# SyncE's transfers in program order, modulation weights loaded beside attention and the FFN's output, and W fetched by DMA in both forms, in a two-layer encoder trunk

## The chip, the core and the metric

The kernel runs on one core of a Trainium2 chip. The metric is the device time of one execution in microseconds (us); less is better. The engines are PE (TensorE), DVE (VectorE), ACT (ScalarE), POOL (GpSimd) and SP (SyncE, which here only issues DMAs). Each engine works through its own instructions in order.

## The reference

Two request groups of 256 tokens each (one row of 512 tokens in the kernel) go through two layers:

```python
mod = silu(c) @ w_mod + b_mod                    # 1024 x 6144 weights per layer; sh1, sc1, gt1, sh2, sc2, gt2
h  = rmsnorm(x, ln1_g) * (1 + sc1) + sh1
q_down, kv_down, rg_x, rg_gate, gdn_qkv, gdn_z, gdn_alpha, gdn_beta, gates = split_cols(h @ w_in)
o_mla, o_rg, o_gdn = attention(q_down, kv_down), rglru(rg_x, rg_gate), gated_delta(gdn_qkv, ...)
x  = x + gt1 * (sum_n sigmoid(gates[n]) * (o_n @ w_branch[n])) @ w_out
h2 = rmsnorm(x, ln2_g) * (1 + sc2) + sh2
x  = x + gt2 * (silu(u_gate) * u_lin) @ ffn_w_down   # u = dwconv(h2 @ ffn_w_up)
```

The gated delta branch (4 heads, both directions, chunks of 64) needs, for each chunk, the inverse T of a unit lower triangular matrix: `T = solve(eye + A, eye)`, then `u = T @ (v * beta)` and `w = T @ (kb * exp(g))`.

## The kernel before

All activations lie feature by token (128 x 512 tiles). Weights are float32; each is split into a rounded part wh and a rest wl, and each product takes three PE passes (hh*wh, hl*wh, hh*wl).

**The weight stream.** The units of all jobs (128x128 weight blocks) lie one behind the other in `wall`; eight units are one chunk of 512 KB. `prefetch` (L375) loads a chunk into one of `NRAW = 3` buffers named raw, `split_chunk` (L381) has ACT cast it to wh (L387) and DVE subtract to wl (L388, recorded as L298), six units before PE needs it. A raw buffer comes free when wl is written.

**The order of the work.** Python code walks the table `BRANCHES` of jobs and writes PE's instructions in that order (`tc.manual_schedule` for PE, L231). A `Driver` keeps a clock `now` that only PE's own work advances. Side tasks are generators: each yields a time to sleep (from `SLACK`) or an event, and `poll` continues those that are due between matmuls. `until(event)` is used where a job must not be written before an event's time: while that time has not come, it runs the tasks that are due and, with none due, puts `now` forward to the next time that a task waits for.

```python
            wakes = [w[0].t if isinstance(w[0], Event) else w[0] for w in self.tasks] + [ev.t]
            wakes = [w for w in wakes if w is not None and w > self.now]
            self.now = min(wakes)
```

Job uk.0 (keys of attention) begins with `drv.until(ev_ckv)`, and that event is set by `ev_ckv.set(SLACK["low_rank_out"])`, which is 152.5. The orders of DVE, ACT, POOL and SP are chosen by a scheduler of the framework, which puts an instruction where it expects it to be ready.

**Modulation (w_mod).** `mod_gen` (L441) computes the columns of mod in groups of blocks: per 512 KB tile, four narrow matmuls with csil (128x32), `PE.matmul(ps..., csil, src)`. Blocks 4 to 9 of a layer (24 tiles) run beside the delta-rule stage; the task is spawned at job close, sleeps `SLACK["mod1"]` for each tile and loads the tile into a raw buffer (L483), so it shares the three buffers and SP with the weight stream. Blocks 10 and 11 are loaded as oraw beside the output projection, blocks 0 and 1 of the next layer run beside the FFN's input (up), and blocks 2 and 3 at the layer's end from tiles hraw that take the place of h.

**The delta-rule stage.** After attention (job close), `GDN.solve` (L1312) runs once per head as a side task. PE computes the Gram matrices (gdn_gram), DVE and POOL make from them B and the diagonal blocks cb. Then a chain of small steps inverts the 16x16 diagonal blocks: SP writes cb to DRAM (dl, L1380) and reads it back in another layout (Lb, four DMAs, L1386); POOL does 30 dependent steps on X (L1387 to L1393; recorded as L292 and L298); SP writes X to DRAM (dx, four DMAs, L1397) and reads it back as W (L1401, L1402); DVE transposes both halves (L1403, L1404). X has one buffer and is set to its start value by a DMA that ACT issues (L1383). The task then sleeps `SLACK["X"]` and `combine` (L1417) has PE build larger blocks (gdn_l16, gdn_l32, gdn_l64), run the recurrence (gdn_rec) and the output (gdn_o).

Of the kernel before, what the change touches and what calls it, by code (L numbers as in the profile page):

```python
# [8 lines left out]
F32 = mybir.dt.float32  # L9
# [4 lines left out]
ALU = mybir.AluOpType  # L14
# [4 lines left out]
P = 128  # L19
T = 512  # L20
# [22 lines left out]
def jobs():  # L43
# [22 lines left out]
    "rg_all": 16.0, "ssq": 6.5, "kq": 8.0, "norm": 2.8, "normed": 17.0, "mod1": 8.0, "mod2": 8.9,  # L66
    "kd": 0.1, "start": 0.6, "diag2": 4.6, "cq": 2.1, "lr_diag": 5.3, "diag": 30.4}
# [159 lines left out]
def body(tc, xT, cT, wall, wmod, pvec, fng, cst, rope, xinit, yT, dbg=None):  # L227
    nc = tc.nc
    es = ExitStack()
    with es:  # L230
        es.enter_context(tc.manual_schedule(engines={mybir.EngineType.PE}))  # L231
        _body(es, tc, nc, xT, cT, wall, wmod, pvec, fng, cst, rope, xinit, yT, dbg)


def _body(es, tc, nc, xT, cT, wall, wmod, pvec, fng, cst, rope, xinit, yT, dbg):
# [36 lines left out]
    V.memset(tiny, 1e-30)  # L272
    dx = [dp.tile([8, P, 32], F32, name=f"dx{i}", tag=f"dx{i}", bufs=1) for i in range(2)]


    def later(pool):
        nc.sync.dma_start(rt_, rope)
        nc.sync.dma_start(fg, fng)
        zero = pool.tile([P, 8, 32], F32, name="zero")
        G.memset(zero, 0.0)  # L280
        for t in dx:
# [93 lines left out]
    def prefetch(at):  # L375
# [61 lines left out]

    def mod_gen(l, groups, pace):  # L441
        if l not in mods:
# [32 lines left out]
        for blocks in groups:  # L475
            n = len(blocks)
            w = 4 // n
            ps = aux_tile(name="mod")
            for i in range(4 * n):
                raw = loaded.pop((l, 4 * blocks[0] + i), None)  # L480
                if raw is None:
                    raw = wp.tile([P, UC * P], F32, name="raw", tag="raw", bufs=NRAW)
                    nc.sync.dma_start(raw, wmod[l, 4 * blocks[0] + i])  # L483
                    yield pace
                half, i4 = divmod(i, 2 * n)
                for e in range(4):
# [7 lines left out]
                yield 0.0  # L494
# [194 lines left out]
    for l in range(depth):  # L689
# [338 lines left out]


        last = l + 1 == depth  # L1030
        for job in JOBS:
            k, *ix = job
            state["job"] = k
            if k == "in6":
# [10 lines left out]
                ev_cq.set(SLACK["cq"])  # L1045
                drv.spawn(low_rank())
            elif k in ("gq", "gk", "gv"):
                if k == "gq" and ix[0] >= 2:
# [23 lines left out]
            elif k == "close":  # L1072
                for t in range(8):
                    debug(f"K{t}_{l}", Kt[:, t, :])
                    debug(f"Q{t}_{l}", Qt[:, t, :])
                fill(mp, 1888)
                mstack.close()
                RT, RS = 8, 2
# [3 lines left out]
                for hd in range(4):  # L1082
                    drv.spawn(gdn.solve(hd))
                drv.spawn(mod_gen(l, ((4, 5, 6, 7), (8, 9)), SLACK["mod1"]))
            elif k == "x":
# [14 lines left out]
            elif k == "mid":  # L1100
                drv.until(gdn.ev_o)
                fill(gdn.g2, 1952)
                g2stack.close()
# [3 lines left out]
            elif k == "close2":  # L1107
# [5 lines left out]

                def oraw(i):
# [3 lines left out]
                preload(l, (10, 11), oraw)  # L1118
                drv.spare.append([0.0, mod_gen(l, ((10, 11),), 0.0)])
            elif k == "out3":  # L1120
# [22 lines left out]
            elif k == "up3":  # L1143
                for n, ps in enumerate(gemms(hs(h2), 3)):
                    up(ps, n)
                if not last:
                    drv.spawn(mod_gen(l + 1, ((0, 1),), SLACK["mod2"]))
            elif k == "up":
                up(gemm(hs(h2)), ix[0])
            elif k == "down":  # L1150
                d, g = ix
                if d == 0:
                    sq = Norm(fp, 3)
                    if not last:
# [3 lines left out]
                        def hraw(i):  # L1158
                            half = []
                            for e in range(2):  # L1160
                                tag = "h%s%d" % ("hl"[e], i % 8)
                                t = hp.tile([P, T], F32, name="hraw", tag=tag)
                                nc.sync.dma_start(t, wmod[l + 1, i][:, e * T:(e + 1) * T])
                                half.append(t)
                            return tuple(half)
                        preload(l + 1, (2, 3), hraw)
                ps = gemm(acts, g)
# [14 lines left out]
        if not last:  # L1182
            drv.spare.append([0.0, mod_gen(l + 1, ((2, 3),), 0.0)])
# [14 lines left out]
class GDN:  # L1198
# [113 lines left out]
    def solve(self, h):  # L1312
# [75 lines left out]
        for j in range(15):  # L1388
# [4 lines left out]
            self.sub(X[:, :, j + 1:], X[:, :, j + 1:], tmp[:, :, :n], G)  # L1393
        dx = self.dx[h % 2]
        for o in range(4):
            e, w = o // 2, 16 * (o % 2)
# [3 lines left out]
        W = g2.tile([P, 2, 2, 4, 32], F32, name="W", tag="W", bufs=1)  # L1400
# [9 lines left out]
        for d in range(2):  # L1410
            self.mul(at[d], at[d], C(inc[d]).unsqueeze(1).to_broadcast([P, 4, P]), G)
        yield SLACK["X"]
        if h:
            yield self.ev_free[h - 1]
# [286 lines left out]
```

## Time and profile before

| | |
|---|---|
| median of 3 runs | 2037.99 us (2036.72 to 2038.59) |
| the profiled execution | 2037.11 us, span from first to last instruction 2035.3 us |
| PE busy | 1956.5 us (96%), mean granted clock 0.978 |
| DVE, ACT, POOL busy | 1246.0, 818.7, 250.9 us |
| DMA | 229.99 MB, mean 113 GB/s |

A busy PE is not a fast PE: the granted clock of a stretch is read beside its busy time. An in-order engine that waits holds everything that is queued behind the waiting instruction, so the views to read are those that say what a queue stood at.

### The profile page before, as it was taken

How to read it: one execution, taken by the hardware profiler on the slowest of the kernel's cores; microseconds unless marked ns; L12 is line 12 of the kernel's file. 1: busy time of each engine (PE TensorE's matmuls, PEld its weight loads, DVE VectorE, ACT ScalarE, POOL GpSimd, SP SyncE). 2: the span in 40 equal slices, each digit the busy share in tenths (PEclk: the TensorE clock that was granted, in tenths of full speed). 3: DMA queues.
4: the chain of work that ended last, by engine and by line, in shares of the span. 5: the costliest groups of instructions: out<-in, count | busy, mean ns of one | idle time of the engine just before them, and what ended most of it. 6: DMA issues, size and time to landing. Idle time of an engine off the chain costs nothing.

```text
span 2035.3 us, 29431 instructions
## 1 busy us (share of the span) xinstructions
PE 1956.5 (96%) x11563; PEld 1568.4 (77%) x11563; DVE 1246.0 (61%) x2354; ACT 818.7 (40%) x1275; POOL 250.9 (12%) x495
## 2 busy tenths in 40 slices
PE   9999977999999999999999998799999999999998
PEld 5777755768888778888878786577788888888887
DVE  5775766745466766663367847685544667666534
ACT  3453454433233444442244533563323344444322
POOL 1100343132100100000011003513130010000000
PEclk9999988999999999999999998899999999999999
DMA  7232333334235343344333123233442633233233
GB/s 300 93 83 69 104 94 89 110 119 120 87 127 185 122 128 102 104 161 127 121 111 113 52 85 104 77 110 91 130 114 82 209 102 103 94 93 104 94 97 111
DMA packets 114138, 229.99 MB, mean 113 GB/s; under 512 B 52304, under 2 KB 57552, under 8 KB 114000
## 3 DMA queue, kind: packets, MB, share of 16 engines
q1 hardware_dynamic: 107376, 219.98, 34.8%
q10 hardware_dynamic: 6624, 8.14, 1.2%
q8 instruction: 91, 1.49, 0.3%
q14 instruction: 47, 0.39, 0.1%
HBM read 221.00 MB, written 7.08 MB: 112 GB/s over the span
## 4 chain that ended last, share of the span: by engine, by line
PE 84%; POOL 5%; DVE 4%; DMA 3%; issue 2%; ACT 1%; SPq 1%; POOLq 0%; DVEq 0%; ACTq 0%
PE mm_up L220 24%; PE mm_down L220 12%; PE mm_gate L220 11%; PE mm_br L220 6%; PE mm_out L220 4%; PE mm_in L220 3%; PE mm_z L220 2%; PE mm_gk L220 2%; PE mod L220 2%; POOL X L298 2%; POOL xt L292 2%; PE mm_gq L220 2%; PE mm_gv L220 2%; PE att_s L220 1%; PE gdn_rec L220 1%
## 5 line engine op out<-in xcount | busy, mean ns | idle before, releaser
L298 DVE TENSOR_TENSOR wl<-raw,wh 128x1024 fp32r<-128x1024 f32 x304 | 375.1, 1234 | 309.7 <-ACT wh L387 296.8
L387 ACT CAST wh<-raw 128x1024 fp32r<-128x1024 f32 x304 | 319.0, 1050 | 539.9 <-PE mm_down L220 129.2
L220 PE MATMUL mm_up<-hh,wh 128*128 128x512 f32 x704 | 276.7, 393 | 3.4 <-POOL hh L308 3.4
L220 PE MATMUL mm_up<-hl,wh 128*128 128x512 f32 x704 | 275.2, 391 | 0.0
L220 PE MATMUL mm_up<-hh,wl 128*128 128x512 f32 x704 | 275.0, 391 | 0.0
L301 DVE SCALAR_TENSOR_TENSOR cv<-mm_up,pv,cv 128x510 f32<-128x510 f32 x176 | 131.2, 748 | 67.9 <-ACT cv L552 64.8
L220 PE MATMUL mm_gate<-hh,wh 128*128 128x512 f32 x384 | 160.6, 418 | 0.0
L220 PEld LDWEIGHTS mm_up<-hh,wh 128*128 128x128 f32 x704 | 132.9, 189 | 34.6 <-POOL hh L308 3.9
L220 PEld LDWEIGHTS mm_up<-hl,wh 128*128 128x128 f32 x704 | 132.9, 189 | 27.8 <-DVE hl L298 0.3
L220 PEld LDWEIGHTS mm_up<-hh,wl 128*128 128x128 f32 x704 | 132.9, 189 | 27.6
L220 PE MATMUL mm_gate<-hh,wl 128*128 128x512 f32 x384 | 150.3, 391 | 0.0
L220 PE MATMUL mm_gate<-hl,wh 128*128 128x512 f32 x384 | 149.9, 390 | 0.0
L220 PE MATMUL mm_down<-ah,wl 128*128 128x512 f32 (+1 forms) x396 | 144.8, 366 | 0.5 <-DVE wl L298 0.5
L220 PE MATMUL mm_down<-ah,wh 128*128 128x512 f32 (+1 forms) x396 | 144.9, 366 | 0.0
L220 PE MATMUL mm_down<-al,wh 128*128 128x512 f32 (+1 forms) x396 | 144.7, 365 | 0.0
L308 POOL TENSOR_SCALAR hh<-hn 128x256 fp32r<-128x256 f32 x64 | 34.1, 545 | 681.2 <-ACT hn L569 678.8
L552 ACT ACTIVATE cv<-mm_up,pv 128x512 f32<-128x512 f32 x88 | 68.5, 780 | 93.7 <-PE mm_up L220 93.7
L220 PEld LDWEIGHTS mm_gate<-hh,wh 128*128 128x128 f32 x384 | 72.2, 188 | 19.5 <-issue 6.5
L220 PEld LDWEIGHTS mm_gate<-hh,wl 128*128 128x128 f32 x384 | 72.1, 188 | 16.3 <-DVE wl L298 0.2
L220 PEld LDWEIGHTS mm_down<-ah,wl 128*128 128x128 f32 x396 | 74.7, 189 | 12.8 <-DVE wl L298 0.7
L220 PEld LDWEIGHTS mm_down<-al,wh 128*128 128x128 f32 x396 | 74.7, 189 | 12.0
L220 PEld LDWEIGHTS mm_down<-ah,wh 128*128 128x128 f32 x396 | 74.7, 189 | 12.0
(388 smaller groups left out, 3853.2 us busy)
## 6 DMA issues: line engine op xcount, KB each, us to landing
raw<-in_wall_dram SPq DMA_DIRECT2D x304, 512.0 KB, 3.5
raw<-in_wmod_dram SPq DMA_DIRECT2D x56, 512.0 KB, 3.7
mraw<-in_wmod_dram SPq DMA_DIRECT2D x16, 512.0 KB, 9.9
oraw<-in_wmod_dram SPq DMA_DIRECT2D x16, 512.0 KB, 6.9
hraw<-in_wmod_dram SPq DMA_DIRECT2D x16, 256.0 KB, 6.1
x<-in_xT_dram SPq DMA_DIRECT2D x8, 256.0 KB, 5.5
xr<-in_xT_dram ACTq DMA_DIRECT2D x8, 256.0 KB, 3.3
xdram<-x ACTq DMA_DIRECT2D x16, 128.0 KB, 2.2
```

The lines of the kernel that those rows point to most:

```text
L220: return self.pe.matmul(out, lhsT, rhs, **kw)
L292: (eng or V).tensor_tensor(out, a, b, ALU.mult)
L298: (eng or V).tensor_tensor(out, a, b, ALU.subtract)
L301: V.scalar_tensor_tensor(out, a, s, b, op0, op1)
L308: G.tensor_scalar(hi, x, 1.0, 0.0, ALU.mult, ALU.add)
L387: A.copy(wh, raw)
L552: A.activation(dst, ps, AF.Identity, bias=bias, scale=w[lo])
```

## The change

Five things, in the words of the code. (1) SP joins PE under the manual order, so its DMAs go out in the order in which the Python code writes them. (2) `split_chunk` loads the chunk two further on. (3) `solve` yields before each of its transfers (cb 4.0, dl 2.5, X 18.0, dx 3.0, W 3.0 in place of X 28.0), so that their place in SP's order is set by the driver's clock; X gets two buffers, and its start value is loaded once per layer (xi) and copied by POOL; POOL also writes a reordered copy XT; X and XT go to two DRAM tensors, and all four parts of W come by DMA, so the two DVE transposes go. (4) The 24 modulation tiles of blocks 4 to 9 go to a task spawned at job in6, beside attention, with a pool of their own of two buffers (mraw) and `SLACK["mod1"]` 5.0; a tile's buffer is reloaded after its matmuls. (5) Blocks 0 and 1 of the next layer move from beside up to beside down, in hraw tiles, with `SLACK["mod2"]` 8.0.

```diff
-    "modev": 0.7, ..., "gram": 3.1, "X": 28.0, ... "mod1": 8.0, "mod2": 8.9,
+    "modev": 0.7, ..., "gram": 3.1, "cb": 4.0, "dl": 2.5, "X": 18.0, "dx": 3.0, "W": 3.0, ... "mod1": 5.0, "mod2": 8.0,
-        es.enter_context(tc.manual_schedule(engines={mybir.EngineType.PE}))
+        es.enter_context(tc.manual_schedule(engines={mybir.EngineType.PE, mybir.EngineType.SP}))
     def split_chunk(at):
             raw = prefetch(at)
             loads.pop(at)
+            l, i = divmod(at[0] * NCH + at[1] + 2, NCH)
+            if l < depth:
+                prefetch((l, i))
+    def modulation(l, groups, pace, tile_of, ahead):
+        todo = [4 * g[0] + i for g in groups for i in range(4 * len(g))]
+        def load():
+            if todo:
+                i = todo.pop(0)
+                loaded[l, i] = tile_of(l, i)
+        for _ in range(ahead):
+            load()
+        return mod_gen(l, groups, pace, load)
-                raw = loaded.pop((l, 4 * blocks[0] + i), None)
-                if raw is None:
-                    raw = wp.tile([P, UC * P], F32, name="raw", tag="raw", bufs=NRAW)
-                    nc.sync.dma_start(raw, wmod[l, 4 * blocks[0] + i])
+                if load is not None:
                     yield pace
+                raw = loaded.pop((l, 4 * blocks[0] + i))
...
+                if load is not None:
+                    load()
+        def mla_raw(l, i):
+            raw = rp.tile([P, UC * P], F32, name="mraw", tag="mraw", bufs=2)
+            nc.sync.dma_start(raw, wmod[l, i])
+            return raw
             if k == "in6":
                 drv.spawn(low_rank())
+                drv.spawn(beside(modulation(l, ((4, 5, 6, 7), (8, 9)), SLACK["mod1"], mla_raw, 2)))
             elif k == "close":
+                drv.until(ev_mod)
-                drv.spawn(mod_gen(l, ((4, 5, 6, 7), (8, 9)), SLACK["mod1"]))
+                gdn.xi = gdn.g2.tile([P, 8, 16], F32, name="xi", tag="xi")
+                nc.sync.dma_start(gdn.xi, xinit)
             elif k == "up3":
-                if not last:
-                    drv.spawn(mod_gen(l + 1, ((0, 1),), SLACK["mod2"]))
             elif k == "down":
-                        preload(l + 1, (2, 3), hraw)
+                        drv.spawn(ahead())
# solve
+        yield SLACK["cb"]
         nc.sync.dma_start(dl.rearrange("t p c -> p t c"), cb)
+        yield SLACK["dl"]
-        X = g2.tile([P, 8, 16], F32, name="X", tag="X", bufs=1)
-        nc.scalar.dma_start(X, self.xinit)
+        X = g2.tile([P, 8, 16], F32, name="X", tag="X", bufs=2)
+        XT = g2.tile([P, 16, 8], F32, name="XT", tag="XT", bufs=1)
+        G.tensor_scalar(X, self.xi, 1.0, 0.0, ALU.mult, ALU.add)
...
-            nc.sync.dma_start(dx.rearrange("t (q s c) i -> s (t q) c i", s=2, c=16)
-                              [o % 2][:, 8 * e:8 * e + 8, w:w + 16], X[32 * o:32 * o + 32])
-        nc.sync.dma_start(W[:, 1, 0], dx[0:4].rearrange("t p c -> p t c"))
-        nc.sync.dma_start(W[:, 0, 1], dx[4:8].rearrange("t p c -> p t c"))
-        V.transpose(W[:, 0, 0], W[:, 1, 0])
-        V.transpose(W[:, 1, 1], W[:, 0, 1])
+        G.tensor_scalar(XT.rearrange("p r c -> p c r"), X, 1.0, 0.0, ALU.mult, ALU.add)
         yield SLACK["X"]
+        for t, (b, n) in zip(dx, ((X, 8), (XT, 16))):
+            for o in range(4):
+                nc.sync.dma_start(v[:, c:c + 8, w:w + 16] if n == 8 else v[:, :, w + c:w + c + 8], b[32 * o:32 * o + 32])
+        yield SLACK["dx"]
+        for i in range(2):
+            nc.sync.dma_start(W[:, 1 - i, 0], dx[i][0:4].rearrange("t p c -> p t c"))
+            nc.sync.dma_start(W[:, i, 1], dx[i][4:8].rearrange("t p c -> p t c"))
+        yield SLACK["W"]
```

Three places in the order of the instructions. The first is PE at job uk.0, in the first layer. Before, the queries (mm_uq) are followed by the keys (mm_uk):

```order
L220 MATMUL mm_uq<-ch,wh 128x512
L220 MATMUL mm_uq<-cl,wh 128x512
L220 MATMUL mm_uq<-ch,wl 128x512
L220 MATMUL mm_uk<-ch,wh 128x512
L220 MATMUL mm_uk<-cl,wh 128x512
L220 MATMUL mm_uk<-ch,wl 128x512
```

In the changed kernel (mod<-mraw are the modulation matmuls, four for each tile):

```order
L220 MATMUL mm_uq<-ch,wl 128x512
L220 MATMUL mod<-mraw,csil 32x256 x56
L220 MATMUL mod_1135<-cs,modev 128x8 x4
L220 MATMUL mod<-mraw,csil 32x256 x24
L220 MATMUL mod_1180<-cs,modev 128x4 x4
L220 MATMUL mm_uk<-ch,wh 128x512
L220 MATMUL mm_uk<-cl,wh 128x512
```

Here 80 modulation matmuls, 20 of the 24 tiles, stand in one run between the two jobs; the other four tiles stand among the jobs before. The second layer has the same run.

The second place is SP at the same point (drope and Qt carry the rotary part of the queries through DRAM). In the changed kernel:

```order
L1053 DMA mraw<-in_wmod_dram 128x1024
L812 DMA drope<-rope 128x1024
L814 DMA Qt<-drope 16x8x512 x2
L1053 DMA mraw<-in_wmod_dram 128x1024 x18
L378 DMA raw<-in_wall_dram 128x1024 x16
```

Eighteen tile loads in a row stand behind Qt; with two buffers each of them waits for the matmuls of the tile two before it.

The third place is SP in the delta-rule stage, the transfers of the second head. Before:

```order
L1380 DMA dl<-cb 128x8x32
L1386 DMA Lb<-dl 32x16x16 x4
L378 DMA raw<-in_wall_dram 128x1024 x2
L483 DMA raw<-in_wmod_dram 128x1024
L1397 DMA dx_93<-X 32x8x16 x4
L378 DMA raw<-in_wall_dram 128x1024
L1401 DMA W<-dx_93 128x4x32
L1402 DMA W<-dx_93 128x4x32
```

In the changed kernel:

```order
L1416 DMA dl<-cb 128x8x32
L1424 DMA Lb<-dl 32x16x16 x4
L378 DMA raw<-in_wall_dram 128x1024 x3
L1448 DMA dx_94<-X 32x8x16 x4
L1448 DMA dx_95<-XT 32x16x8 x4
L1452 DMA W<-dx_94 128x4x32
L1453 DMA W<-dx_94 128x4x32
L1452 DMA W<-dx_95 128x4x32
L1453 DMA W<-dx_95 128x4x32
```

Three weight chunks instead of two go out between Lb and dx, no modulation tile stands there, and twelve small transfers take the place of six.

## Rows read from the trace of the kernel before

**Rows 1.** The page's second part, PE in 40 slices of the span.

```profile
PE   9999977999999999999999998799999999999998
```

**Rows 2.** Windows of 25 us: length, then busy PE, PEld, DVE, ACT, POOL, PEclk, DMA.

```profile
250.00:275.00 25.00, 18.30 (x144) 14.40 (x144) 13.06 (x29) 11.82 (x20) 5.19 (x15) 0.80 0.26 74
275.00:300.00 25.00, 21.40 (x243) 14.46 (x241) 20.88 (x42) 15.81 (x27) 15.31 (x26) 0.93 0.36 96
300.00:325.00 25.00, 12.86 (x80) 9.92 (x80) 13.34 (x17) 9.21 (x12) 12.49 (x23) 0.81 0.30 78
```

**Rows 3.** The same in windows of 5 us, around the two longest waits.

```profile
260.00:265.00 5.00, 0.00 (x0) 0.00 (x0) 2.33 (x8) 1.45 (x3) 0.00 (x0) 0.60 0.92 293
265.00:270.00 5.00, 4.81 (x16) 4.21 (x16) 2.63 (x5) 1.80 (x3) 0.00 (x0) 0.50 0.09 34
...
320.00:325.00 5.00, 1.42 (x6) 1.42 (x7) 3.02 (x5) 3.95 (x5) 0.00 (x0) 0.50 0.53 139
```

**Rows 4.** Waits, all engines: total us, times, longest.

```profile
DVE W L1403 <- DMA W<-dx: 77.9, 8, 13.3
```

**Rows 5.** Waits of SP's queue.

```profile
SPq L1397 <- POOL X L298: 84.6, 8, 12.7
```

**Rows 6.** The chain that ended last, 205 to 350 us: start, length, what.

```profile
222.24 0.57 PE mod L220 x8
...
233.86 2.24 DMA dl<-cb
...
271.44 0.68 PE gdn_l L220 x50
...
335.38 0.68 PE gdn_l L220 x50
```

**Rows 7.** Timeline in the two waits; in brackets the idle time before and its releaser.

```profile
256.31 1.80 SPq L1397 DMA_DIRECT2D dx<-X  x4
...
259.75 0.60 ACT L1339 ACTIVATE E<-gdn_z 128x512 f32<-128x512 f32 x1 [4.99 <-DMA dx<-X]
...
262.59 0.31 DVE L1403 STREAM_TRANSPOSE W<-W 128x128 f32<-128x128 f32 x1 [8.62 <-DMA W<-dx]
263.55 0.31 DVE L1404 STREAM_TRANSPOSE W<-W 128x128 f32<-128x128 f32 x1
...
320.07 1.04 ACT L387 CAST wh<-raw 128x1024 fp32r<-128x1024 f32 x1 [13.05 <-DMA raw<-in_wall_dram]
...
321.99 0.31 DVE L1404 STREAM_TRANSPOSE W<-W 128x128 f32<-128x128 f32 x1 [0.98 <-DMA W<-dx]
...
323.58 0.80 PE L220 MATMUL gdn_rec<-Ss,kq 128*128 128x128 f32 x2 [11.25 <-ACT Ss L1510]
```

**Rows 8.** Timeline at job uk.0, PE and SP.

```profile
96.73 0.39 PE L220 MATMUL mm_uk<-ch,wh 128*128 128x512 f32 x1
...
101.31 0.33 SPq L793 DMA_DIRECT2D drope<-rope  x1
...
104.32 0.90 SPq L795 DMA_DIRECT2D Qt<-drope  x2
```

**Rows 9.** DMA issues: size, median us from issue to landing.

```profile
raw<-in_wmod_dram SPq DMA_DIRECT2D x56, 512.0 KB, 3.7
...
dx<-X SPq DMA_DIRECT2D x32, 16.0 KB, 1.6
```

**Rows 10.** Landing of raw loads: the whole span, and the one beside Qt.

```profile
DMA to landing us min/median/max: 3.3/3.6/11.0
...
DMA to landing us min/median/max: 4.6/4.6/4.6
```

**Rows 11.** Timeline of one modulation tile and the load that takes its buffer.

```profile
222.17 0.64 PE L220 MATMUL mod<-raw,csil 128*32 128x256 f32 x8
222.87 0.33 SPq L378 DMA_DIRECT2D raw<-in_wall_dram  x1
```

**Rows 12.** Window of 2 us in the start; the last number is GB/s.

```profile
10.00:12.00 2.00, 1.96 (x10) 0.69 (x7) 2.00 (x8) 1.56 (x3) 0.00 (x0) 1.00 1.05 422
```

More of the change, by code (lines that the diff above doesn't have):

```diff
@@ L63 @@
     "rg_x": 0.8, "ab": 5.7, "softplus": 13.7, "gates": 4.7, "v": 5.8, "ws": 3.0, "z": 0.2, "gw":
[1 row of a table removed]
[1 row of a table added]
     1.8, "Y": 2.5, "v1": 3.6, "S": 0.8, "r": 2.9, "v2": 5.1, "on": 1.7, "o": 35.8, "rope": 1.5,
-    "rg_all": 16.0, "ssq": 6.5, "kq": 8.0, "norm": 2.8, "normed": 17.0, "mod1": 8.0, "mod2": 8.9,
+    "rg_all": 16.0, "ssq": 6.5, "kq": 8.0, "norm": 2.8, "normed": 17.0, "mod1": 5.0, "mod2": 8.0,
     "kd": 0.1, "start": 0.6, "diag2": 4.6, "cq": 2.1, "lr_diag": 5.3, "diag": 30.4}
@@ L272, in _body @@
     V.memset(tiny, 1e-30)
-    dx = [dp.tile([8, P, 32], F32, name=f"dx{i}", tag=f"dx{i}", bufs=1) for i in range(2)]
+    dx = [[dp.tile([8, P, 32], F32, name=f"dx{i}{j}", tag=f"dx{i}{j}", bufs=1) for j in range(2)] for i in range(2)]
     def later(pool):
@@ L280, in later @@
         G.memset(zero, 0.0)
-        for t in dx:
+        for t in dx[0] + dx[1]:
             nc.sync.dma_start(t.rearrange("t p c -> p t c"), zero)
@@ L436, in preload, with mod_gen @@
             loaded[l, 4 * blocks[0] + i] = tile_of(4 * blocks[0] + i)
-    def mod_gen(l, groups, pace):
+    def modulation(l, groups, pace, tile_of, ahead):
[7 more added lines that the diff above has]
+        return mod_gen(l, groups, pace, load)
+    def mod_gen(l, groups, pace, load=None):
         if l not in mods:
@@ L491, in mod_gen @@
                               stop=(k >= 8 - w), tile_position=(0, 32 * q))
+                if load is not None:
+                    load()
                 if i == 1 and waiting:
                     select()
-                yield 0.0
+                if load is None:
+                    yield 0.0
             ev = sp.tile([P, T], F32, name="modev", tag="modev", bufs=1)
@@ L705, in _body @@
         M2 = 10
+        rstack = ExitStack()
+        rp = rstack.enter_context(tc.tile_pool(name="mraw", bufs=1))
         gdn = GDN(nc, tc, locals())
@@ L1027, in up, with beside, next_raw, ahead @@
             uv.clear()
+        ev_mod = drv.event()
+        def mla_raw(l, i):
+            raw = rp.tile([P, UC * P], F32, name="mraw", tag="mraw", bufs=2)
+            nc.sync.dma_start(raw, wmod[l, i])
+            return raw
+        def beside(gen):
+            yield from gen
+            ev_mod.set(0.0)
+        def next_raw(l, i):
+            half = []
+            for e in range(2):
+                t = hp.tile([P, T], F32, name="hraw", tag="h%s%d" % ("hl"[e], i % 8))
+                nc.sync.dma_start(t, wmod[l, i][:, e * T:(e + 1) * T])
+                half.append(t)
+            return tuple(half)
+        def ahead():
+            yield from modulation(l + 1, ((0, 1),), SLACK["mod2"], next_raw, 8)
+            drv.spare.append([0.0, modulation(l + 1, ((2, 3),), 0.0, next_raw, 8)])
         last = l + 1 == depth
@@ L1075, in _body @@
                     debug(f"Q{t}_{l}", Qt[:, t, :])
+                drv.until(ev_mod)
                 fill(mp, 1888)
+                rstack.close()
                 mstack.close()
@@ L1101, in _body @@
                 drv.until(gdn.ev_o)
-                fill(gdn.g2, 1952)
+                fill(gdn.g2, 416)
                 g2stack.close()
@@ L1112, in _body, with oraw @@
                 sq = Norm(op_, 3)
-                def oraw(i):
+                def oraw(l, i):
                     raw = rp.tile([P, UC * P], F32, name="oraw", tag="oraw", bufs=8)
@@ L1117, in oraw @@
                     return raw
-                preload(l, (10, 11), oraw)
-                drv.spare.append([0.0, mod_gen(l, ((10, 11),), 0.0)])
+                drv.spare.append([0.0, modulation(l, ((10, 11),), 0.0, oraw, 8)])
             elif k == "out3":
@@ L1156, in _body @@
                         xdram = dp.tile([P, 8, T], F32, name="xdram", tag="xdram")
[L1158 to L1165, printed above, removed]
-                        preload(l + 1, (2, 3), hraw)
+                        drv.spawn(ahead())
                 ps = gemm(acts, g)
@@ L1182, in _body @@
         if not last:
-            drv.spare.append([0.0, mod_gen(l + 1, ((2, 3),), 0.0)])
             wait(SLACK["norm"])
@@ L1393, in solve @@
             self.sub(X[:, :, j + 1:], X[:, :, j + 1:], tmp[:, :, :n], G)
-        dx = self.dx[h % 2]
-        for o in range(4):
-            e, w = o // 2, 16 * (o % 2)
-            nc.sync.dma_start(dx.rearrange("t (q s c) i -> s (t q) c i", s=2, c=16)
-                              [o % 2][:, 8 * e:8 * e + 8, w:w + 16], X[32 * o:32 * o + 32])
-        W = g2.tile([P, 2, 2, 4, 32], F32, name="W", tag="W", bufs=1)
-        nc.sync.dma_start(W[:, 1, 0], dx[0:4].rearrange("t p c -> p t c"))
-        nc.sync.dma_start(W[:, 0, 1], dx[4:8].rearrange("t p c -> p t c"))
-        V.transpose(W[:, 0, 0], W[:, 1, 0])
-        V.transpose(W[:, 1, 1], W[:, 0, 1])
+        G.tensor_scalar(XT.rearrange("p r c -> p c r"), X, 1.0, 0.0, ALU.mult, ALU.add)
         Y = [g2.tile([P, 4, P], F32, name="Y", tag="Y", bufs=2) for _ in range(2)]
@@ L1412, in solve @@
         yield SLACK["X"]
+        dx = self.dx[h % 2]
+        for t, (b, n) in zip(dx, ((X, 8), (XT, 16))):
+            for o in range(4):
+                w = 16 * (o % 2)
+                v = t.rearrange("t (q s c) i -> s (t q) c i", s=2, c=16)[o % 2]
+                c = 8 * (o // 2)
+                nc.sync.dma_start(v[:, c:c + 8, w:w + 16] if n == 8 else v[:, :, w + c:w + c + 8], b[32 * o:32 * o + 32])
+        yield SLACK["dx"]
+        W = g2.tile([P, 2, 2, 4, 32], F32, name="W", tag="W", bufs=1)
+        for i in range(2):
+            nc.sync.dma_start(W[:, 1 - i, 0], dx[i][0:4].rearrange("t p c -> p t c"))
+            nc.sync.dma_start(W[:, i, 1], dx[i][4:8].rearrange("t p c -> p t c"))
+        yield SLACK["W"]
         if h:
```

2 rows, old and new, of the table SLACK are left out of this document.

## The prediction

> **What bounds the kernel now.** I read the page's slices first. PE is full in most of the span; its row dips in the same two places of each layer [rows 1]: slices 6 and 7 (254 to 356 us) and slices 26 and 27 repeat each other one layer apart, so I work out one layer and double it. The windows of 25 us put sizes on the dip: from 250 to 325 us PE is busy 18.3, 21.4 and 12.9 of 25 us, so 22.4 us are idle, and the granted clock is down to 0.80 and 0.81 in two of the three [rows 2]. The windows of 5 us show what follows a wait: after a stretch with nothing on PE, and in one with 1.42 us of work in 5, the clock is at 0.60 and 0.50, the latter being the 1.2 GHz level, and it stays there into the next work (4.81 us busy at 0.50) [rows 3]. Half of that work's time is lost, so some 2.5 us after each long wait. Together the stage loses about 22.4 + 2 x 2.5 = 27 us per layer. Elsewhere there is little to win: the FFN's slices all read 9, 90% or more [rows 1].
>
> The waits say why. Three in-order queues stand still for the delta-rule chain and hold back what is behind it: SP stands at the dx transfers for POOL's X (84.6 us in 8 waits, up to 12.7) [rows 5], DVE at its transpose for W (77.9 us in 8 waits, up to 13.3) [rows 4], and ACT once for dx, because its reload of X needs the one buffer of X [rows 7]. In the second wait the weights pay for it: ACT gets its chunk 13.05 us late, and PE waits 11.25 us for an ACT copy that stands behind that cast [rows 7].
>
> **The change part by part.**
>
> *SP's order, weights two ahead, X with two buffers, W without transposes.* These take exactly those blocks away: the two transposes leave DVE (0.31 us each, their wait up to 9 us [rows 7]), ACT's reload leaves ACT, and weight chunks are sent before dx rather than behind it. What is late next is W itself, since PE stands in order at gdn_l. That chain grows: SP issues eight dx transfers instead of four and four W transfers instead of two. Four dx took 1.80 us of issue [rows 7], so the eight and the two more W take some 2.7 us of issue more, of which the W half that needs X alone hides about 1; and XT's runs are half as long and twice as many, so they land after between the 1.6 us of dx [rows 9] and, as an estimate, twice that. Against that the transposes go, 0.6 us. I take 2.5 us more from X to W (bounds 1 to 4).
>
> Head 0: its chain runs from 233.86 (dl) to W complete at 263.9, and PE comes to gdn_l at 271.44 [rows 6, 7]. PE lost some 6.7 us idle [rows 2] and 2.5 us of clock on the way, and four modulation tiles of 0.57 us [rows 6] also go. So PE would arrive near 260 and find W at about 266. The wait does not vanish, it moves to PE's own queue, but DVE and ACT run on through it.
> Head 1: before, W is complete at 322.3 [rows 7] and PE reaches gdn_l at 335.38 [rows 6]; without the seven modulation tiles that stood on the way that is 331.4. In the changed kernel DVE no longer loses 8.6 us behind W of head 0 [rows 7], so head 1's chain starts about 9 us sooner (bounds 0 and 13): W at 322.3 + 2.5 - 9 = 315.8. PE, without the second wait (11.3 us) and the first, would be there before. So gdn_l moves from 331.4 to 315.8, 15.6 us; the later heads' waits are of W and stay. **Gain: 16 us per layer.** Lower bound: the chain starts no sooner, 331.4 - 324.8 = 7. Upper bound: everything that the stage loses, 27.
>
> *Modulation beside attention.* The title has it beside attention at a pace of 5 us. The order shows otherwise. Job uk.0 first asks the driver to reach ev_ckv's time, 152.5 after low_rank; the driver jumps its clock forward and runs whatever is due on the way, and now the modulation task is due every 5 us of that jump. So 20 of the 24 tiles are written in one run between the last query and the first key, with no other matmul between them, and 18 of their loads stand in a row on SP behind Qt. Before, the same jump found no such task and cost nothing.
>
> What the run takes: PE reaches mm_uk at 96.73 today [rows 8]. In the changed kernel four tiles stand before that, then tiles 5 and 6 lie in the two buffers, then PE waits. SP can't send the seventh tile before Qt, which goes out from 104.32 to 105.2, because drope needs DVE's rope at 101.31 [rows 8]. From there two buffers go round: a load lands 3.7 us after its issue [rows 9], the tile's matmuls take 0.64 us and SP issues 0.06 us after them [rows 11], so a turn of two tiles is 4.4 us with PE at 2.4 GHz. PE would be busy about 1.3 us in such a turn, which is nearest to the row of 1.42 us in 5 at 0.50 [rows 3], so I take its matmuls at 1.2 GHz, 1.28 us, and a turn of 5.0 us. Nine turns make 45 us. The second tile of the last turn, ACT's copy and the last select add an estimated 3 us. PE then reaches uk.0 at 105.2 + 45 + 3 = 153.2 instead of 96.7, 56.5 us later; the 24 tiles no longer stand later in the layer (24 x 0.57 = 13.7 us [rows 6]), which leaves 42.8 us, and the next work starts at the low clock, 2.5 us [rows 3]. **Price: 45 us per layer.** Nothing covers it: PE is in order, and all that is behind uk.0 waits. Bounds: a landing of 3.3 us [rows 10] at the full clock gives turns of 4.0 us and a price of 34; one of 4.6 us, as that of the load sent beside Qt [rows 10], at the low clock gives turns of 5.9 us and 53.
>
> For the landing, the Trainium skill has a rule that differs from the row: DMA: Bandwidth & Descriptors, section Anatomy of one DMA, fits 2.0 us plus the bytes over 436 GB/s for GpSimd's path, an estimate of 3.2 us for 512 KB. By it a turn would be 0.5 us shorter and the whole sum 9 us less in two layers; the row of SP's own queue, 3.7 us [rows 9], decides here.
>
> *Blocks 0 and 1 beside down instead of up, oraw, hraw.* Eight tiles of 0.57 us move from one stretch where PE is full to another: nothing. Their loads come eight ahead, in tiles that up has finished with; if that cover failed, one landing of 3.7 us would show, once.
>
> *The weight stream in the FFN.* Three buffers, each reloaded when wl is written, as before: nothing.
>
> **The sum.** Per layer +45 - 16 = +29 us, twice: +58 us. The profiled execution took 2037.1 us, 0.9 us below the median of 2038.0. So 2037 + 58 = **2095 us**. Bounds: 2 x (34 - 27) = +14 and 2 x (53 - 7) = +92, 2051 to 2129.
>
> **The rivals.**
> (a) *PE's wait for W takes back the whole gain.* The four yields of the solve task add up to 30.5 where 28 stood, but the measured chain of head 0 alone is 30 us from dl to W, before the extra transfers, and cb comes late from DVE. If no chain starts sooner, the gain is 7 or less: 2037 + 2 x (45 - 7) = 2113 us. For it: PE stands at gdn_l in any case. Against: DVE's 77.9 us of waits are gone [rows 4].
> (b) *The stage runs without a wait and the run of tiles is at its cheapest.* Gain 27, price 34: 2051 us. For it: all three blocks are removed. Against: head 0's W is still later than PE.
> (c) *Faster: the tile loads are limited by bytes, not by landing.* The engines have moved 422 GB/s [rows 12], at which a tile takes 1.24 us; 18 tiles take 22.4 us. If two loads in flight reach that rate, the first lands at 108.9 and the run ends at about 134: price 134 - 96.7 - 13.7 = 24 us. With the gain at its bound of 27 that is 2 x (-3) = 2031 us. The point from which it decides is the turn: with 16 us gained, the price must fall below 16, a turn of less than 2 us for two tiles; with 27 gained, a turn of 3.2 us. Against: 422 GB/s came with many loads queued, and here a buffer's load can't go out before its matmuls; the shortest landing alone is 3.3 us [rows 10].
> (d) *The change doesn't do what it says*: modulation beside attention would be hidden work on a full PE and cost nothing, and the kernel would gain 16 x 2, some 2005 us. That needs other matmuls between the 20 tiles, and the order has none. I give it nothing of its own.
>
> **How the numbers follow.** Forecast (price 38 to 51, gain 10 to 22: 2069 to 2119) 0.72, the figure 2095; (a) 0.12; (b) 0.10; (c) 0.04; 0.02 for something between (b) and (c). A difference under 0.2%, 4 us, can't be told from none here; only cases between (b) and (c) fall there. So faster 0.04, same 0.02, slower 0.94. The range holds the forecast's cases and most of (a) and (b): 2055 to 2126.
>
> **What the changed profile would show.** Right: PE with little work and a granted clock near 0.5 from about 101 to 153 us and again one layer on (near 1125 to 1180 us), its waits there put to DMA of mraw; turns of about 5 us for two tiles; no wait of DVE at W, no X reload on ACT; PE waits at gdn_l for W in heads 0 and 1; 250 to 350 us (shifted by some 45) with less idle. Wrong, if uk.0 follows the queries within 35 us, if the tiles come faster than one per 2 us, if the delta-rule stage is as idle as now, or if a stretch of the FFN shows PE waiting for weights.

## The result and the profile after

The changed kernel takes **2115.48 us** (median of 4 runs, 2112.62 to 2115.99) against 2038.29 us for the kernel before (2036.72 to 2038.61): a ratio of **1.0386**, 95% interval 1.0369 to 1.0404. The forecast was 2095, with a range of 2055 to 2126. The profiled execution took 2115.39 us, with a span of 2113.6 us at a mean granted clock of 0.953; before, the span was 2035.3 us. So 78.3 us have to be found.

The page's slices, PE and its clock (each slice is 52.8 us), show where to look. They answer to [rows 1]; slices are counted from 1.

```profile
PE   9939998999999999999996699979999999999998
PEclk9959999999999999999998599989999999999999
```

The old dips in slices 6 and 7 and in 25 and 26 are smaller: an 8 in slice 7 and a 7 in slice 27 are left of them. A new hole stands in slice 3 and again in slices 22 and 23, one layer apart, with the clock down to 5 tenths. The windows of 25 us put a size on it (length, then busy PE, PEld, DVE, ACT, POOL, PEclk, DMA share, GB/s):

```profile
100.00:125.00 25.00, 6.90 (x59) 1.50 (x57) 3.63 (x5) 0.00 (x0) 0.00 (x0) 0.58 0.58 167
125.00:150.00 25.00, 11.96 (x88) 3.80 (x88) 0.58 (x6) 0.58 (x1) 0.00 (x0) 0.50 0.62 196
150.00:175.00 25.00, 18.67 (x90) 13.06 (x83) 5.22 (x10) 5.01 (x7) 0.00 (x0) 0.69 0.37 121
```

In the first two windows DVE, ACT and POOL have next to nothing to do, and in the second PE is at its 1.2 GHz level throughout (0.50). What PE does there is in its timeline (in brackets the idle time before and its releaser):

```profile
100.41 1.07 PE L220 MATMUL mod<-mraw,csil 128*32 128x256 f32 x16
113.71 2.29 PE L220 MATMUL mod<-mraw,csil 128*32 128x256 f32 x16 [12.23 <-DMA mraw<-in_wmod_dram]
118.60 1.08 PE L220 MATMUL mod<-mraw,csil 128*32 128x256 f32 x8 [2.60 <-DMA mraw<-in_wmod_dram]
120.34 1.08 PE L220 MATMUL mod<-mraw,csil 128*32 128x256 f32 x8 [0.66 <-DMA mraw<-in_wmod_dram]
123.38 1.08 PE L220 MATMUL mod<-mraw,csil 128*32 128x256 f32 x8 [1.96 <-DMA mraw<-in_wmod_dram]
...
154.97 1.08 PE L220 MATMUL mod<-mraw,csil 128*32 128x256 f32 x8 [1.54 <-DMA mraw<-in_wmod_dram]
158.32 1.08 PE L220 MATMUL mod<-mraw,csil 128*32 128x256 f32 x8 [2.27 <-DMA mraw<-in_wmod_dram]
160.16 1.87 PE L220 MATMUL mod<-cs,modev 128*128 128x4 f32 x8 [0.76 <-ACT modev L513]
161.89 0.78 PE L220 MATMUL mm_uk<-ch,wh 128*128 128x512 f32 x1
```

This is the run of 20 tiles: eight matmuls of 1.08 us in all, an idle stretch for the next load, and so on, until uk.0 starts at 161.89 us; before it started at 96.73 [rows 8]. From 113.71 to 154.97 are eight turns of two tiles, 5.16 us each. SP's timeline of the same stretch has the loads in a row behind Qt; answering to [rows 8]:

```profile
103.66 0.33 SPq L812 DMA_DIRECT2D drope<-rope  x1
106.27 0.80 SPq L814 DMA_DIRECT2D Qt<-drope  x2
107.17 46.65 SPq L1053 DMA_DIRECT2D mraw<-in_wmod_dram  x18
```

The page's DMA issues, the median from issue to landing in the last number, answer to [rows 9]:

```profile
raw<-in_wall_dram SPq DMA_DIRECT2D x304, 512.0 KB, 3.6
mraw<-in_wmod_dram SPq DMA_DIRECT2D x64, 512.0 KB, 4.2
oraw<-in_wmod_dram SPq DMA_DIRECT2D x16, 512.0 KB, 7.1
```

PE's waits (total us, times, longest):

```profile
PE mod L220 <- DMA mraw<-in_wmod_dram: 73.0, 32, 12.3
PE mm_x L220 <- DVE wl L298: 11.9, 2, 6.0
PE gdn_l L220 <- DMA W<-dx: 7.5, 2, 4.8
```

and SP's:

```profile
SPq L1416 <- DVE cb L1412: 115.6, 8, 22.9
SPq L1448 <- POOL X L298: 72.9, 8, 12.8
```

DVE's wait at W [rows 4] has gone, and so has ACT's for dx. SP still stands at X (72.9 us in 8 waits where [rows 5] has 84.6), and it now stands long at dl's source cb (115.6). The delta-rule stage is better: its two emptiest windows hold 19.03 and 20.86 us of work, where the two emptiest of [rows 2] held 18.30 and 12.86.

```profile
325.00:350.00 25.00, 19.03 (x228) 14.37 (x227) 23.68 (x46) 16.02 (x23) 13.18 (x21) 0.86 0.41 89
350.00:375.00 25.00, 20.86 (x170) 16.21 (x169) 22.82 (x36) 21.18 (x34) 17.40 (x32) 0.98 0.23 54
```

Head 1's last transfer of W, which landed 2.2 us after its issue, and PE's first use of that W, without a wait:

```profile
374.51 0.51 SPq L1453 DMA_DIRECT2D W<-dx  x1
381.57 0.75 PE L220 MATMUL gdn_l<-W,B 32*32 32x32 f32 x64
```

**Where the time went.** All of it can be read from the starts of a few jobs on PE. Each layer is cut at gq.1 (where the attention ends), at the first matmul of the last branch (where the delta rule ends), at the first out and at the first up. Layer 0, in us, for the kernels of this study; the experiments follow (differences of starts, good to 0.1 us):

| kernel | start to gq.1 | gq.1 to last branch | out to up | up to next layer |
|---|---|---|---|---|
| before | 212.6 | 368.5 | 54.5 | 380.0 |
| after | 278.7 | 338.6 | 55.6 | 380.3 |
| e1_no_jump | 230.8 | 339.7 | 56.2 | 381.5 |
| e3_half_jump | 255.2 | 341.8 | 55.9 | 380.5 |
| e4_transposes | 230.9 | 343.4 | 55.6 | 380.0 |
| e5_one_ahead | 239.4 | 340.0 | 62.0 | 380.1 |
| e6_before_W_dma | 211.2 | 377.1 | 55.0 | 380.4 |
| e7_tiles_back | 219.4 | 350.8 | 55.8 | 380.7 |
| e8_slack | 231.2 | 342.1 | 57.0 | 380.2 |
| e9_rope_later | 212.8 | 353.9 | 55.6 | 380.1 |

In layer 0 uk.0 comes 65.2 us later, and the work from uk.0 to gq.1 takes 1.0 more; in layer 1 (counted from its first in6) 66.7 and 2.3. Less 13.7 us for the 24 tiles that no longer stand further on, the run's price is 52.5 and 55.3 us. The delta-rule stage is 29.9 us shorter, of which 13.7 are those tiles: a gain of 16.2 us, and 15.3 in layer 1. The output stage costs 1.2 and 1.0 us more. Together 107.8 - 31.5 + 2.2 = 78.5 us, against 78.3 measured; the FFN and the end take up the rest. The 13.7 are the prediction's 0.57 us for each tile; e9_rope_later, further on, prices the tiles in that stage at 14.2, which would move 0.5 us per layer from the one term to the other.

### The profile page after: what moved, and what is told of

The parts are those of the page before. It is cut to its first block, busy times and chain, and to the rows that moved or that the text cites. A ratio compares the mean times of both kernels' runs of the same rounds, so it can differ in the third digit from the quotient of the medians.

```text
span 2113.6 us, 29530 instructions
## 1 busy us (share of the span) xinstructions
PE 1976.4 (94%) x11563; PEld 1580.1 (75%) x11563; DVE 1246.3 (59%) x2338; ACT 817.0 (39%) x1275; POOL 256.7 (12%) x511
## 4 chain that ended last, share of the span: by engine, by line
PE 80%; DVE 7%; DMA 6%; ACT 2%; issue 2%; POOL 1%; SPq 1%; DVEq 0%; ACTq 0%; POOLq 0%
PE mm_up L220 23%; PE mm_down L220 11%; PE mm_gate L220 10%; PE mm_br L220 6%; DMA mraw<-in_wmod_dram 4%; PE mm_in L220 3%; PE mm_out L220 3%; PE mod L220 2%; PE mm_gk L220 2%; PE mm_gq L220 2%; PE mm_gv L220 2%; PE mm_g L220 1%; PE att_s L220 1%; PE gdn_rec L220 1%; PE mm_z L220 1%
## 5 line engine op out<-in xcount | busy, mean ns | idle before, releaser
L220 PE MATMUL mod<-mraw,csil 128*32 128x256 f32 x512 | 56.3, 532 | 73.2 <-DMA mraw<-in_wmod_dram 73.0
L220 PEld LDWEIGHTS mod<-mraw,csil 128*32 128x32 f32 x512 | 12.3, 128 | 112.2 <-DMA mraw<-in_wmod_dram 102.3
```

The source lines that it names most:

```text
L220: return self.pe.matmul(out, lhsT, rhs, **kw)
```

## The experiments

The theory: the run of tiles, written by the driver's jump at uk.0, is the whole loss, and what is left of the change is a gain. The rival: tiles beside attention, or SP's program order, cost the same wherever they are written.

**e1_no_jump: no jump of the driver.**

```diff
-    "low_rank": 11.8, "low_rank_out": 152.5,
+    "low_rank": 11.8, "low_rank_out": 5.0,
```

> The changed kernel with low_rank_out 5.0 in place of 152.5, so that the driver's clock does not jump before job uk.0 and the 24 modulation tiles stand between attention's matmuls, some 5 us apart. Theory (the price is the run of 20 tiles written by the jump, 52 to 55 us per layer): 2115 - 2 x 54 = 2007 us, faster than the kernel before by the gain of the delta-rule stage; no wait of PE for mraw over 2 us. Rival (attention, with PE full and the weight stream on the same queue, can't carry the 24 loads wherever they stand): the waits spread over the stage and the time stays above 2070 us.

Measured: 2024.57 us (2022.65 to 2026.23), ratio to before 0.9943 (0.9926 to 0.9959). With that number the tiles stand one by one among the attention's matmuls, as the timeline of PE in e1_no_jump shows:

```profile
132.25 0.39 PE L220 MATMUL mm_gv<-hl,wh 128*128 128x512 f32 x1
132.48 0.39 PE L220 MATMUL mm_gv<-hh,wl 128*128 128x512 f32 x1
132.79 0.64 PE L220 MATMUL mod<-mraw,csil 128*32 128x256 f32 x8
133.36 0.66 PE L224 MATMUL att_t<-cs,pt 128*128 128x128 f32 x4
```

The hole is gone; the same windows of e1_no_jump:

```profile
100.00:125.00 25.00, 24.20 (x126) 17.11 (x125) 13.82 (x18) 10.36 (x15) 0.00 (x0) 1.00 0.72 232
125.00:150.00 25.00, 25.00 (x147) 17.93 (x149) 22.40 (x68) 13.93 (x44) 0.00 (x0) 1.00 0.31 106
```

One number undone turns a loss of 3.9% into a gain of 0.6%, and PE waits for mraw 0.9 us at the longest in the attention: the theory holds in the main, and the rival's figure, above 2070 us, falls. In the kernel before, the same edit leaves every instruction on PE, SP and DVE in its place, so the jump cost nothing there. But the time is 17 us above the 2007 that the theory gave. Between the profiled executions, where the run's 107.8 us should have gone, 15.1 are missing, and the starts of the jobs show where: the attention is 18.2 us longer than before (22.8 in layer 1), where 13.7 were reckoned for the tiles, which is 4.5 + 9.1 = 13.6; the FFN takes 2.3 us more than in the changed kernel, and the delta-rule stages together take 1.2 less. So a part of the rival stays: tiles beside attention cost more than reckoned. e7 and e9 take it up.

**e3_half_jump: half the jump.** The same number at 60.0, which leaves a run of ten tiles.

> The changed kernel with low_rank_out 60.0: 10 tiles in the run instead of 20. Theory (the price is two-buffer turns, about 2.6 us for each tile of the run, after one wait for the loads behind Qt): 10 tiles fewer x (2.6 to 2.9 us, less the 0.57 us they cost elsewhere) = 20 to 24 us less per layer, 2068 to 2075 us. Rival (the price is the one long wait behind Qt and the low clock after it, whatever the number of tiles): 2105 to 2115 us.

Measured: 2074.29 us (one run; span 2072.5). PE's timeline:

```profile
111.86 2.28 PE L220 MATMUL mod<-mraw,csil 128*32 128x256 f32 x16 [12.28 <-DMA mraw<-in_wmod_dram]
...
129.28 1.08 PE L220 MATMUL mod<-mraw,csil 128*32 128x256 f32 x8 [1.68 <-DMA mraw<-in_wmod_dram]
130.29 0.80 PE L220 MATMUL mm_uk<-ch,wh 128*128 128x512 f32 x1
```

uk.0 starts 31.6 us earlier than in the changed kernel. The spans of none, ten and twenty tiles in the run are 2020.9, 2072.5 and 2113.6: some 26 and 21 us per layer for each ten, the first ten with the wait of 12.28 us for the first load behind Qt. The price goes by the tile, with that one wait in the first ten. That more than two buffers would make a turn shorter was not tried.

**e4_transposes: W's two transposes back, on e1_no_jump.**

```diff
-        for t, (b, n) in zip(dx, ((X, 8), (XT, 16))):
+        for t, (b, n) in zip(dx, ((X, 8),)):
...
+        V.transpose(W[:, 0, 0], W[:, 1, 0])
+        V.transpose(W[:, 1, 1], W[:, 0, 1])
```

> e1 with W's other halves made again by the two DVE transposes (four dx and two W transfers, no XT). Theory (DVE standing at W was a good part of what the delta-rule stage lost): DVE waits at W for some 70 us in 8 waits again and the time is 2018 to 2028 us, half of the gain gone. Rival (the gain comes from SP's order and the weights two chunks ahead; DVE's wait at W is covered, and eight small transfers fewer even help): 2003 to 2009 us, same as e1 or below it.

Measured: 2030.75 us, ratio 0.9970 (0.9959 to 0.9982), 0.3% or some 6 us above e1_no_jump and just above the theory's range. DVE's and PE's waits in e4_transposes:

```profile
DVE W L1451 <- DMA W<-dx: 41.6, 8, 8.1
```
```profile
PE gdn_rec L220 <- DVE r L295: 9.7, 2, 5.1
```

DVE stands at W again, half as long as before [rows 4], where the theory had some 70 us, and PE at what DVE does behind it. The delta-rule stage is 3.8 us longer than in e1_no_jump, and 6.0 in layer 1; the spans differ by 5.2 us. So of the stage's gain in e1_no_jump, 15.1 and 17.5 us, some 4 and 6 are W by DMA. The rest came with what this run keeps: SP's written order, X in two buffers and set by POOL, the tiles elsewhere and the weights two ahead. e5 and e9 below show that a gain stays without either of the last two; the order and X's buffers were not taken apart.

**e6_before_W_dma: that part alone, on the kernel before.** W in both forms by DMA, X with two buffers and copied by POOL; SP's order left to the scheduler, weights and tiles as before.

```diff
-        X = g2.tile([P, 8, 16], F32, name="X", tag="X", bufs=1)
-        nc.scalar.dma_start(X, self.xinit)
+        X = g2.tile([P, 8, 16], F32, name="X", tag="X", bufs=2)
+        XT = g2.tile([P, 16, 8], F32, name="XT", tag="XT", bufs=1)
+        G.tensor_scalar(X, self.xi, 1.0, 0.0, ALU.mult, ALU.add)
...
-        V.transpose(W[:, 0, 0], W[:, 1, 0])
-        V.transpose(W[:, 1, 1], W[:, 0, 1])
```

> The kernel before with the third part alone: all of W by DMA, X in two buffers set by POOL from xi, no ACT reload, no DVE transposes; SP still in the scheduler's order, modulation as before. Theory (the three blocks each cost; SP's at dx stays here): 2020 to 2030 us. Rival (only SP's order counts): 2035 to 2045 us, not faster than before, as SP has six transfers more per head with the weights behind them.

Measured: 2051.8 us, ratio 1.0078 (1.0062 to 1.0093). Slower, and neither side had that. PE's and ACT's waits in e6_before_W_dma:

```profile
PE gdn_l L220 <- DMA W<-dx: 29.0, 6, 6.6
PE mm_b L220 <- ACT rs L912: 25.2, 2, 12.8
```
```profile
ACT wh L387 <- DMA raw<-in_wall_dram: 113.7, 18, 13.2
```

Here PE does stand at gdn_l for W, as the prediction said of the changed kernel. ACT waits longer for weights in total than before (80.0 us in 17), but PE's long wait for ACT is not new. In the kernel before it stood at another matmul, also behind a cast that came 13 us late [rows 7]:

```profile
PE gdn_rec L220 <- ACT Ss L1510: 21.9, 2, 11.2
```

So W by DMA moved DVE's stand at W to PE and left the late chunk where it was. From the first dx to W complete it took 9.7 and 10.0 us in the first two heads, where the kernel before took 7.6 and 8.1 with the transposes. The delta-rule stage takes 377.1 us where it took 368.5. That the chunks come late because they stand behind twelve small transfers of a head instead of six is argued from the order; no run shows it alone.

**e5_one_ahead: weights one chunk ahead instead of two, on e1_no_jump.**

```diff
-            l, i = divmod(at[0] * NCH + at[1] + 2, NCH)
+            l, i = divmod(at[0] * NCH + at[1] + 1, NCH)
```

> Edit: on top of e1_no_jump (the driver's jump taken out), the weight chunk issued at each split is the next one instead of the one after it. Theory (in SP's program order a chunk stands behind SP's waits for cb and X of the delta rule, 22.9 and 11.1 us at the longest in e1_no_jump, and only the second chunk ahead covers them): with one chunk ahead the weights come late in the delta-rule stage, ScalarE waits for raw from DMA and TensorE for wl; each of 8 heads loses some 2 to 6 us: 2040 to 2070 us. Rival (the gain of the stage came from the transposes and the order alone, a chunk of 13 us of matmuls being cover enough): within 5 us of e1_no_jump, 2020 to 2030 us.

Measured: 2047.48 us, ratio 1.0064 (1.0040 to 1.0089): some 1.2% above e1_no_jump. The size is the theory's, the place is not. The delta-rule stage takes 340.0 us, as with two ahead; the loss is in the attention (+8.6 us) and in the output stage (+5.9). PE's waits name the jobs:

```profile
PE mm_out L220 <- ACT wh L391: 9.3, 2, 4.9
PE mm_gk L220 <- ACT wh L391: 8.7, 2, 4.6
```

These are the places where SP's order puts drope and Qt, or eight tile loads, in front of a chunk. The second chunk covers those; the stands at cb and X, 165.4 and 120.2 us here, cost the stage 0.3 us more with one chunk ahead (1.2 in layer 1).

**e7_tiles_back: the 24 tiles back in the delta-rule stage, on e1_no_jump.**

```diff
-                drv.spawn(beside(modulation(l, ((4, 5, 6, 7), (8, 9)), SLACK["mod1"], mla_raw, 2)))
...
+                drv.spawn(modulation(l, ((4, 5, 6, 7), (8, 9)), SLACK["mod1"], mla_raw, 1))
                 gdn.xi = gdn.g2.tile([P, 8, 16], F32, name="xi", tag="xi")
```

> Edit: on top of e1_no_jump, the 24 tiles of w_mod go back to where the kernel before had them, into the delta-rule stage (paced by 8 us, loaded one ahead into the weights' three buffers), nothing beside attention. Theory (a tile beside attention costs TensorE 0.75 to 0.95 us, a tile in the delta-rule stage lies partly in TensorE's waits, 19 us of them a layer in e1_no_jump): attention becomes 18 to 22 us a layer shorter, the delta-rule stage 8 to 20 us longer: 2005 to 2024 us. Rival (the tiles' loads take a weight buffer each and SP waits for it, so weights come late as in e6_before_W_dma): 2030 to 2055 us.

Measured: 2018.71 us (2011.28 to 2022.35), ratio 0.9910 (0.9875 to 0.9945). The theory's total holds, but not its first term: the attention is only 11.4 us shorter (13.7 in layer 1) where 18 to 22 were expected, the delta-rule stage 11.2 longer (14.4). With no tile in it the attention still takes 219.4 us, 6.8 more than before. PE's and SP's waits in e7_tiles_back, the first from 60 to 220 us, the second over the span:

```profile
PE mm_uk L220 <- ACT wh L391: 4.8, 1, 4.8
```
```profile
SPq L812 <- DVE rope L298: 28.9, 2, 15.0
```

SP stands at drope until DVE has the rope, and a chunk of weights is behind it.

**e9_rope_later: drope and Qt written 7 us later, on e7_tiles_back.**

```diff
-                dr = dp.tile([P, 2, T], F32, name="drope", tag="drope")
-                nc.sync.dma_start(dr, x)
+                def send():
+                    yield 7.0
+                    dr = dp.tile([P, 2, T], F32, name="drope", tag="drope")
+                    nc.sync.dma_start(dr, x)
...
+                drv.spawn(send())
```

> Edit: on top of e7_tiles_back, the transfers of drope and Qt are written 7 us later, so that two weight chunks go out on SP in front of them. In e7_tiles_back SP stands 14 to 15 us at drope for VectorE's rope, and TensorE then waits 4.8 us a layer at mm_uk for ScalarE's cast of a chunk that stood behind it. Theory (what SP's program order still costs in attention is this one stand): attention some 5 to 7 us a layer shorter, the rest as it was: 2003 to 2012 us. Rival (Qt is then late for the attention's first scores, or SP's other stands take its place): 2014 to 2030 us.

Measured: **2006.31 us** (2000.74 to 2011.8), ratio **0.9854** (0.9833 to 0.9874), the fastest here, and faster than both kernels of the change. All that PE waits for from 60 to 230 us:

```profile
PE mm_uv L220 <- ACT Vt L840: 0.7, 1, 0.7
PE mm_gq L220 <- DVE rope L292: 0.6, 1, 0.6
```

The attention is back at 212.8 us, and the delta-rule stage, with its tiles in it as before, takes 353.9 instead of 368.5, 14.6 us less (17.2 in layer 1); with the output stage's 1.2 and 0.7 us more that is 29.9 of the 30.5 us between the spans, 2035.3 and 2004.8. The rest was not quite as it was: in layer 0 the delta-rule stage takes 3.1 us more than in e7_tiles_back. This also prices a tile: between e9_rope_later and e1_no_jump the 24 tiles change place, and they cost 14.2 us in the delta-rule stage (0.59 each) and 18.0 and 23.0 us in the attention of the two layers (0.75 and 0.96; in layer 1 one window of 25 us is at a clock of 0.93). SP's stand at drope is in e1_no_jump too, 6.4 us in layer 0, but PE's waits among the attention's matmuls are 0.9 us at most there, so it is not in this price.

**e8_slack: a miss.** On e1_no_jump, dl written 14 us after cb instead of 4, and four tiles ahead of the output stage instead of eight.

```diff
-    "cb": 4.0,
+    "cb": 14.0,
...
-                drv.spare.append([0.0, modulation(l, ((10, 11),), 0.0, oraw, 8)])
+                drv.spare.append([0.0, modulation(l, ((10, 11),), 0.0, oraw, 4)])
```

> Edit: on top of e1_no_jump, dl's transfers are written 14 us after cb's program instead of 4, so that SP stands at cb for less time, and four instead of eight tiles of the attention output's w_mod blocks are loaded ahead of that stage's weights. Theory (SP's stands at cb are what makes wl late, 6.0 us a layer, and the eight tiles in front of the first weights of the output stage cost 1.2 us a layer): 2008 to 2021 us. Rival (SP's stands are covered by two chunks, and dl comes later to the delta rule): 2022 to 2040 us.

Measured: 2031.02 us, ratio 0.9975 (0.9961 to 0.9988), 0.3% above e1_no_jump: the rival. The delta-rule stage is 2.5 us longer and the output stage 0.8. SP's wait at cb for DVE fell from 115.6 to 6.5 us, and PE's longest wait in the stage is the same as in the changed kernel:

```profile
PE mm_x L220 <- DVE wl L298: 11.9, 2, 5.9
```

So SP's stands at cb are not what makes wl late there. The trace of the changed kernel shows what does, in the first of these waits:

```profile
333.31 1.05 ACT L391 CAST wh<-raw 128x1024 fp32r<-128x1024 f32 x1 [1.48 <-PE mm_g L220]
345.25 1.30 DVE L298 TENSOR_TENSOR wl<-raw,wh 128x1024 fp32r<-128x1024 f32 x1
346.61 0.80 PE L220 MATMUL mm_x<-hh,wl 128*128 128x512 f32 x1 [5.97 <-DVE wl L298]
```

The cast was done at 334.36, and DVE, busy for 10.68 of the 10.80 us from 334.40 to 345.20, did other work of its queue first. The chunk was there in time; its place in DVE's order was late. That another order of DVE would take the wait away was not tried.

## Why the prediction was right, and where it was not

- **The time: right, with two errors in it.** At 2115 us it lies in the forecast's own case, 2069 to 2119, though the price lies above that case's 51 in both layers. By the number alone it would be rival (a)'s 2113; the stage's gain of 16 us, not 7, tells them apart.
- **The run of tiles: right in kind, 7 to 10 us per layer too cheap.** PE idle and at a clock near 0.50 from 101 us on, waits put to mraw, a turn of two tiles near 5 us, the same one layer on: all as forecast. The price was put at 45 and measured 52.5 and 55.3, beyond the upper bound of 53 in layer 1. The mis-sized term is the start and end of the run in "105.2 + 45 + 3 = 153.2", which came out at 161.9. Qt's issue ended 1.9 us later than reckoned. The first tile behind it came 6.6 us after that, not 3.7 (+2.9). Eight turns were 5.16 us, not 5.0 (+1.3). From the 19th tile to uk.0 it took 6.9 us, not 4.3 (+2.6). That is 8.7 us. The low clock behind the run, taken as 2.5 us, cost 1.0 and 2.3.
- **The landing.** The row of 3.7 us was chosen against the estimate of 3.2 from the Trainium skill (DMA: Bandwidth & Descriptors, Anatomy of one DMA), which is made for GpSimd's path. The median of the loads in question is 4.2 us, further from the page than the row was.
- **The gain of the delta-rule stage: right.** 16 us were forecast, 16.2 and 15.3 measured. Neither the stage without waits (27, rival b) nor the gain taken back (7, rival a) came.
- **"What is late next is W itself": wrong.** PE was to stand at gdn_l for W in heads 0 and 1. It waits there 7.5 us in 2 waits in the whole execution, both in the last head of a layer, and the single longest wait of the stage is mm_x for DVE's wl, 6.0 us. Two terms were mis-sized. From X to W was to take 2.5 us more (bounds 1 to 4); from the first dx to W complete the first two heads took 8.1 us, where 7.6 and 8.1 stood, so 0 to 0.5 more. It grew by 2 only in e6_before_W_dma, in the scheduler's order. And head 1's chain was to start 9 us sooner; counted from gq.1, its dl went out 11.8 us sooner. So W of head 1 was complete 98.0 us after gq.1, where 103.2 was forecast (315.8 - 212.6), and PE came to it 4.8 us after that, at 102.8, having worked all that time at a mean clock of 0.59. The size came out in part by luck, from a W that was early and a PE that was late.
- **The order's share.** The prediction treated order, X's buffers and W as one gain. The runs take W apart from the rest: W by DMA gives 3.8 us of 15.1 in the stage (6.0 of 17.5 in layer 1) on top of the order and X's buffers (e4_transposes), and loses 0.8% on the kernel before (e6_before_W_dma).
- **A tile's price: too low.** 0.57 us for each tile is its own length. Among the attention's matmuls it costs 0.75 us and more (e1_no_jump against e9_rope_later). In the changed kernel the error hardly shows, as 20 of the 24 tiles stand in the run; in e1_no_jump, 24 times some 0.19 us are 4.6 us per layer, 9 of the 15 that it lacks.
- **Slices.** The second dip was read as slices 26 and 27; counted as the first one it is 25 and 26.
- **"Three in-order queues": one was missed.** Program order on SP was costed where the tiles stand and in the delta-rule stage, and not at drope and in front of the output stage. In the changed kernel the stand at drope lies right ahead of the run and can't be told from it; e7_tiles_back against e9_rope_later shows it as 6.6 us in layer 0 and 6.8 in layer 1, where another 2.6 went before uk.0, at a mean clock of 0.91 against 1.00 in the layer's first 36 us. The output stage, 1.2 and 1.0 us, was costed at nothing.
- **FFN: right.** From up to the next layer 380.0 us before, 380.3 after.
- **Rival (c), loads limited by bytes: fell.** From 125 to 150 us the loads moved 196 GB/s against the 422 of [rows 12]; a turn takes 5.16 us, far above the 2 to 3 from which that rival would decide. **Rival (d)**, tiles as hidden work at 2005 us, fell too: even one by one (e1_no_jump) they cost more than their own length in the attention.

## What to carry to other kernels

Where a planner's clock decides the written order, print the order after adding a paced task: one jump of that clock, harmless as long as nothing was due in it, put 20 tiles in a row, and one number took the time from 1.039 of before to 0.994. Where transfers are written in program order on one queue, look at each transfer that waits for a computed value and ask which weight stands behind it; writing one such transfer two chunks later took the time from 0.991 to 0.985 of before. A number among the waits of a queue, as the 115.6 us at cb, is no cost until an engine on the path is shown waiting behind it.

## What the runs showed that was not expected

A load of 512 KB takes 3.6 us to land as a rule in the weight stream, 4.2 us when two of them go round with two buffers, 7.1 us when eight are sent at once (medians of the page), and the first behind Qt took 6.6 us from the end of Qt's issue to its matmuls. In the run of tiles the granted clock stayed at 0.50 for 25 us at a time with PE busy for 11.96 of 25 us, so that a tile took 1.08 us instead of 0.64. A tile of eight small matmuls costs the attention 0.75 to 0.96 us, more than its own 0.57 to 0.64. The timeline of PE in the changed kernel shows the rest at the edges:

```profile
89.13 0.39 PE L220 MATMUL mm_uq<-ch,wl 128*128 128x512 f32 x1
89.45 0.64 PE L220 MATMUL mod<-mraw,csil 128*32 128x256 f32 x8
90.02 0.50 PE L220 MATMUL mm_uq<-ch,wh 128*128 128x512 f32 x1
90.35 0.39 PE L220 MATMUL mm_uq<-cl,wh 128*128 128x512 f32 x1
```

From start to start, a matmul of this job takes 0.23 us. The one ahead of the tile takes 0.32, the tile 0.57 and the one behind it 0.33: 0.76 us for the tile, and 24 of them are 18.2. That it is less in the delta-rule stage, 0.59, fits a PE that has waits there to hide a part; this is argued and not shown.
